# Attention outputs kept in SBUF, a weight ring of three, and the last two gate tiles computed plainly

## The chip, the core and the metric

The kernel runs on one core of a Trainium2 chip. TensorE (PE) does the matmuls, ScalarE (ACT) and VectorE (DVE) the elementwise work beside it, GpSimd (POOL) some elementwise work and DMA issue, and SyncE (SP) issues most DMAs; SP's queue is called SPq in the rows. The metric is the device time of one execution in microseconds (us), as a median of repeated runs.

## The reference

Sequence length S is 512, model width 2048 (16 chunks of 128), all float32. Two layers of a first block are followed by one layer of a second. Cut to what this case touches:

```python
for l in range(2):                                   # first block
    h = rmsnorm(x, attn_norm_g[l])
    qa, ka, va, ga, cq, ckv, kr, gb = split(h @ w_in[l])
    ya = swa_attention(qa, ka, va, sinks[l]) * silu(ga)      # 16 heads, window 128
    yb = mla_attention(cq, ckv, kr, ...) * silu(gb)          # 8 heads of 128
    x = x + concat([ya, yb]) @ w_out[l]
x = rmsnorm(x, final_norm_g)
# second block, 16 meta tokens in front
q, k, v, g_attn, u, g_pool, m_attn, m_pool = split(rmsnorm(hs) @ w_in_2)
o_attn = stick_breaking_attention(q, k, v) * silu(g_attn)
o_pool = (pool(u) @ pool_w) * pool_scale * silu(g_pool)
merged = sigmoid(m_attn) * (o_attn @ w_attn_up) + sigmoid(m_pool) * (o_pool @ w_pool_up)
out = rmsnorm(hs + merged @ w_out_2)
```

## The kernel before

Activations lie transposed: a tile holds 128 features by 512 positions. Every float32 product is made of three matmuls: each operand is split into a high part (a CAST on ACT, names ending in h) and a low part (a subtract on DVE, names ending in l), and `mm3` adds high x high, high x low and low x high. A plain output tile of 128 features takes two weights (halves of the contraction) of 8 chunks each, so 2 x 24 matmuls of 512 columns.

**Weights.** `next_w` keeps two split weights ahead of PE. SP loads each weight (128x1024) into the ring `wr` (four buffers, L179), ACT casts it into `wh` (three buffers), DVE writes `wl` (three buffers). A load into `wr` has to wait until the subtract that reads the old content is done; that subtract follows the cast, and the cast waits until PE has left the weight three places back. SP issues in program order, so a DMA that stands behind a weight load waits with it.

**Slots.** Nearly every other tile comes from one pool, `slots`, of 74 buffers of 128x528.

**Order.** The order in which the program issues work is the order on each engine. GEMMs run as the main line; attention heads (`mla_head`, `swa_pair`) are generators that are stepped between matmuls (`tick`), by a running estimate of PE's time. `SEQ1` lists the tiles of a layer of the first block: after cq, ckv, kr come the eight multi-head-latent heads (tiles gb), whose outputs are called yb (chunks 0 to 7), then ka, va, and the eight sliding-window pairs: a projection qa0, then qa(i), ga(i-1) in turn, then ga7. Pair i is started after qa(i); it computes scores (sc) and probabilities p, transposes them (tp), splits them (pTh, pTl), multiplies with v (o) and, when gate ga(i) is there, copies two halves to `ya` (L531), adds the rest and multiplies by the gate: chunk 8 + i.

`ydst` (L754) sends chunks 0 to 13 of y to DRAM (`yd`) on POOL's queue; only the last two stay. `yget` (L760) reads a chunk back into a tile `yr` through SP, and splits it. It is called for y0 to y7 after ga4 to ga7, two each, and for y8 to y15 when the output projection first needs them. The output projection computes its first three tiles as a group: first half of the contraction (y0 to y7) for three tiles, then the second half (y8 to y15) for three tiles.

**Second block.** `SEQ2`: heads, pool tiles, then the gates ma and mp. Two neighbouring gate tiles are one `run_pair` (L312): seven products of 24 matmuls with 256 columns each (in z, x and y), in place of the 2 x 48 of 512 of two plain tiles. Four of the seven weights are sums of weight blocks that POOL's DMAs made earlier in DRAM (`wsd`, `sum_step`, 16 pairs). The gate's sigmoid (sga) goes to DRAM (`sgd`). The chunks o0 to o15 of the heads and the pool lie in DRAM (`od`); `o_load` (L1110) reads one through SP and splits it. o0 to o7 are loaded after the last pair's matmuls are issued, o8 to o15 behind the pair's gates. Then au(i) (needs o0 to o7) and pu(i) (needs o8 to o15) follow, one weight each.

Of the kernel before, what the change touches and what calls it, by code (L numbers as in the profile page):

```python
# [18 lines left out]
P = 128  # L19
# [16 lines left out]
POOL_W = (2, 4, 8, 16)  # L36

GRP = 3
NSLOT = 74
HN = S // 2  # L40
SUMPAIRS = NC
NSIDE = 3
TP_WAIT = 4000

# [53 lines left out]
def trunk_kernel(ctx, tc, xT, w_in, w_qkv, w_out, w_in2, w_pool, w_aup, w_pup, w_out2, metaT, vec, cst, outT):  # L98
# [9 lines left out]
    def slot(name, dt=F32, cols=S):  # L108
        t = slots.tile([P, W], dt, tag="s", name=name)
        return t[:, :cols]  # L110
# [64 lines left out]
    wq = deque()  # L175
    wready = deque()

    def w_raw(src, n, tag="wr", bufs=4):
        raw = wp.tile([P, WCOLS], F32, tag=tag, name=tag, bufs=bufs)[:, :n]  # L179
        nc.sync.dma_start(raw, src)  # L180
        return raw
# [233 lines left out]
        nc.sync.dma_start(diag_t, cst[:, C_DIAG:C_DIAG + S])  # L415

    xd = [tc.dram_tile([P, NC, S], F32, name=f"xd{i}") for i in range(2)]
    yd = [tc.dram_tile([P, NC, S], F32, name=f"yd{i}") for i in range(2)]

    def split_g(x, g, name):  # L420
        hi = slot(name + "h", F32R)
# [30 lines left out]
    def swa_pair(i, qps, r, st, nsink, gate, ydst):  # L452
        qf = slot("qf")
        stt(qf, qps, 0.125, r, ALU.mult, ALU.mult)
        qs_t = []
        for kv in range(2):
            t = slot("qs", F32R)
            on = slice(kv * 64, kv * 64 + 64)
            off = slice(64 - kv * 64, 128 - kv * 64)
            split(qf[on], "", hi=t[on], lo=t[off])  # L460
            qs_t.append(t)
        al = slot("alibi")
        for kv in range(2):
            nc.gpsimd.tensor_scalar(al[:, kv * 256:(kv + 1) * 256], delta_t, -SLOPES[kv * 8 + i], None, op0=ALU.mult)
        yield 4500
        while "vz" not in st:
            yield 500
        kz, vz = st["kz"], st["vz"]
        nm = small.tile([P, 8], F32, tag="nm", name="nm")
        rs = small.tile([P, 8], F32, tag="rs", name="rs")  # L470
        es = small.tile([P, 8], F32, tag="es", name="es")
        pts = []
        for b in range(NB):
            sc = ps_at("sc")
            c0 = P if b == 0 else 0
            qs = slice(b * P, (b + 1) * P)
            ks = slice(max(b - 1, 0) * P, (b + 1) * P)
            pt = slot("p")
            for kv in range(2):
                kh, kl = kz[kv]  # L480
                js = slice(kv * 256 + c0, kv * 256 + 256)
                mm2(sc[:, js], qs_t[kv][:, qs], kh[:, ks], kl[:, ks], True, True)
            for kv in range(2):
                js = slice(kv * 256 + c0, kv * 256 + 256)
                j = 2 * b + kv
                nc.vector.tensor_tensor_reduce(pt[:, js], sc[:, js], al[:, js], -1.0, nsink[:, 2 * i + kv:2 * i + kv + 1],  # L486
                                               ALU.add, ALU.min, nm[:, j:j + 1])
                act(pt[:, js], pt[:, js], AF.Exp, bias=nm[:, j:j + 1], scale=-1.0, accum_out=rs[:, j:j + 1])
            pts.append(pt)
            yield 1200  # L490
        sk = nsink[:, 2 * i:2 * i + 2].unsqueeze(1).to_broadcast([P, NB, 2])
        tt(es.rearrange("p (b k) -> p b k", k=2), nm.rearrange("p (b k) -> p b k", k=2), sk, ALU.subtract)
        act(es, es, AF.Exp)
        tt(rs, rs, es, ALU.add)
        nc.vector.reciprocal(rs, rs)
        for b in range(NB):
            c0 = P if b == 0 else 0
            v = pts[b].rearrange("p (h k) -> p h k", k=256)[:, :, c0:256]
            nc.vector.tensor_tensor(v, v, rs[:, 2 * b:2 * b + 2].unsqueeze(2).to_broadcast([P, 2, 256 - c0]), ALU.mult)
        yield 4000  # L500
        o = [ps_at("o"), ps_at("o")]
        todo = []

        def pv(j, nq, th, tl, first):
            for kv in range(2):
                cs = slice(kv * nq * P, (kv + 1) * nq * P)
                mm2(o[kv][:, j * P:(j + nq) * P], vz[kv][:, j, :], th[:, cs], tl[:, cs], first, j == 3)

        for j in (0, 2, 1, 3):
            nq = 2 if j < 3 else 1  # L510
            tp = ps_at("tp")
            th = slot("pTh", F32R)
            tl = slot("pTl", F32R)
            for kv in range(2):
                for a in range(nq):
                    src = pts[j + a][:, kv * 256 + (1 - a) * P:kv * 256 + (2 - a) * P]
                    transp(tp[:, (kv * nq + a) * P:(kv * nq + a + 1) * P], src)
            n = 2 * nq * P
            split(tp[:, :n], "", hi=th[:, :n], lo=tl[:, :n])
            if todo:  # L520
                pv(*todo.pop())
            todo.append((j, nq, th, tl, j == 0))
            yield TP_WAIT
        pv(*todo.pop())
        while ("a", i) not in gate:
            yield 500
        y = slot("ya")
        for kv in range(2):
            on = slice(kv * 64, kv * 64 + 64)
            off = slice(64 - kv * 64, 128 - kv * 64)  # L530
            nc.scalar.copy(y[on], o[kv][off])  # L531
            tt(y[on], o[kv][on], y[on], ALU.add)
        nc.gpsimd.tensor_tensor(y, y, gate.pop(("a", i)), ALU.mult)
        ydst(8 + i, y)

    def lora_norm(pss, gcol, name, res):

# [73 lines left out]
    def mla_head(h, pr, kr, gate, ydst):  # L611
# [51 lines left out]
            yield 500  # L663
        y = slot("yb")
        tt(y, o, gate.pop(("b", h)), ALU.mult)
        ydst(h, y)

    def grouped(w, t0, n):
        for u in range(2):
# [3 lines left out]
    def plan():  # L673
# [23 lines left out]
        for kind, i in SEQ2:  # L697
            if kind == "pw":
                wq.append((w_pool[i], 512))
            elif kind == "au":  # L700
                wq.append((w_aup[i], WCOLS))
            elif kind == "pu":
                wq.append((w_pup[i], WCOLS))
            elif kind in ("ma", "mp"):
                if i % 2 == 0:
                    blocks = (w_in2[t, 0], w_in2[t, 1], w_in2[t + 1, 0], w_in2[t + 1, 1])
                    wq.extend((src, WCOLS) for src in pair_steps(len(pairs), *blocks))
                    pairs.append(blocks)
                t += 1
            else:  # L710
                for u in range(2):
                    wq.append((w_in2[t, u], WCOLS))
                t += 1
# [24 lines left out]
    def layer(lay, h, rd, x_src, x_dst):  # L738
# [12 lines left out]
        y = [None] * NC  # L751
        ys = [None] * NC

        def ydst(c, t):  # L754
            if c < NC - 2:
                nc.gpsimd.dma_start(yd[lay][:, c, :], t)
                t = True
            y[c] = t

        def yget(c):  # L760
            if ys[c] is None:
                need(lambda: y[c] is not None)
                t = y[c]
                if t is True:
                    t = slot("yr")
                    nc.sync.dma_start(t, yd[lay][:, c, :])
                ys[c] = split(t, f"y{c}")
                y[c] = None
            return ys[c]

# [5 lines left out]
        for kind, i in SEQ1:  # L776
# [18 lines left out]
            elif kind == "pb":  # L795
                mla_proj_b(st["cqn"], st["ckvn"], proj[i])
                tick()
            elif kind == "pc":
                pr = proj.pop(i)
                mla_proj_c(st["ckvn"], pr)  # L800
                for hh in range(2):
                    start_side(mla_head(2 * i + hh, pr, kr, gate, ydst), 6000 + 3000 * hh)
            elif kind == "ka":
                ka = scaled("kaf")
            elif kind == "va":
                start_side(swa_prep(ka, scaled("vaf"), st))
            elif kind == "qa":
                start_side(swa_pair(i, run_gemm(2, 8, hget), rd["r"], st, nsink, gate, ydst))
            elif kind == "ga":
                gate["a", i] = gate_silu(run_gemm(2, 8, hget), rd["r"], "ga")  # L810
                if i >= 4:
                    yget(2 * i - 8)
                    yget(2 * i - 7)

        sq = SumSq("x")
        if lay == 1:
# [303 lines left out]
    for kind, i in SEQ2:  # L1120
# [21 lines left out]
        elif kind == "pw":  # L1142
            wh, wl = next_w()
            rhs = [pooled.pop(2 * i), pooled.pop(2 * i + 1)]
            for d in range(2):
# [5 lines left out]
                stt(t, ps, vcol(V_PSC + 2 * i + d), gates.pop(("p", 2 * i + d)), ALU.mult, ALU.mult)  # L1151
                nc.sync.dma_start(od[:, SB + 2 * i + d, :], t)
        elif kind in ("ma", "mp"):
            if i % 2:
                continue
            if not oo:
                need(lambda: len(done) == SB)
                oo = [None] * (2 * SB)
            at = i + (0 if kind == "ma" else NC)
            c = run_pair(tset, 8)  # L1160
            if (kind, i) == ("mp", NC - 2):
                X2 = tset = None
                for k in range(SB):
                    oo[k] = o_load(k)
            for d, t in enumerate(pair_out(c, sr)):
                nc.scalar.dma_start(sgd[:, at + d, :], gate_sigmoid(t, "sg"))
            if X2 is None:
                for k in range(SB, 2 * SB):
                    oo[k] = o_load(k)
        elif kind == "au":  # L1170
            ya = slot("ym")
            ga = sg_load(i)
# [180 lines left out]
```

## Time and profile before

| | |
|---|---|
| median of 3 runs | 2760.93 us (2760.64 to 2765.09) |
| the profiled execution | 2759.14 us, span 2757.4 us |
| granted PE clock, mean over the span | 0.991 of full speed |
| busy share of the span | PE 97%, DVE 58%, ACT 44%, POOL 18% |
| DMA traffic | 395.81 MB, 144 GB/s on average |

The span runs from the first to the last instruction of the profiled execution; times in rows are counted from its start. A matmul's duration in the rows includes its way through the array, so the distance from one start to the next is the rate. In a row of the timeline, [2.40 <-ACT pTh L137] says that the engine was idle for 2.40 us before it and that the cast to pTh ended the wait.

### The profile page before, as it was taken

What the parts mean: (1) busy time and instruction counts of PE and PEld (TensorE: products, weight loads), DVE (VectorE), ACT (ScalarE), POOL (GpSimd) and SP (SyncE); (2) the same over time, 40 slices, a digit from 0 to 9 for tenths busy, and PEclk for the clock granted to TensorE, in tenths of its full rate; (3) what the DMA queues carried; (4) which work ended last, traced back from release to release, by engine and by line L of the source; (5) the groups of instructions that cost most, each with busy time, mean ns of one, the idle gap of its engine ahead of it and who ended that gap; (6) DMA issues with size and microseconds to landing.
All of it is one profiled execution on the core that took longest, in us unless ns stands there. A gap on an engine that the chain in (4) does not pass through costs nothing.

```text
span 2757.4 us, 37840 instructions
## 1 busy us (share of the span) xinstructions
PE 2688.1 (97%) x14809; PEld 2315.0 (84%) x14809; DVE 1605.9 (58%) x2399; ACT 1217.0 (44%) x2021; POOL 507.9 (18%) x461
## 2 busy tenths in 40 slices
PE   8999999899999999999999999999999999899997
PEld 6888888688788888877888989898899999688886
DVE  7767567544476756655554444547566666544445
ACT  5445455432344445553334433443346666422232
POOL 4121132222111213223411111111220000011112
PEclk9999999999999999999999999999999999999998
DMA  5354554567654554557632222223346666644334
GB/s 182 114 142 131 138 140 139 168 199 206 174 135 134 141 136 138 150 149 196 188 114 76 77 79 82 70 77 118 100 138 218 208 215 212 199 143 143 120 121 130
DMA packets 129410, 395.81 MB, mean 144 GB/s; under 512 B 14400, under 2 KB 18880, under 8 KB 129232
## 3 DMA queue, kind: packets, MB, share of 16 engines
q1 hardware_dynamic: 103568, 309.90, 35.1%
q0 software_dynamic: 20912, 75.04, 12.5%
q10 hardware_dynamic: 4752, 8.46, 0.8%
q8 instruction: 116, 1.90, 0.3%
q14 instruction: 62, 0.51, 0.1%
HBM read 360.84 MB, written 99.61 MB: 167 GB/s over the span
## 4 chain that ended last, share of the span: by engine, by line
PE 51%; issue 2%; DVE 2%; ACT 1%; POOL 1%; DMA 1%; SPq 0%; DVEq 0%; POOLq 0%; ACTq 0%
PE mm L146 27%; PE mmA L146 5%; PE y L146 5%; PE mmB L146 5%; PE x L146 3%; PE z L146 3%; ACT sp L129 1%; PE so L146 1%; POOL suf L989 0%; DMA ol<-od 0%; DVE out L1231 0%; POOL suf L988 0%; PE pw L146 0%; DVE sufl L122 0%; DMA yr<-yd 0%
## 5 line engine op out<-in xcount | busy, mean ns | idle before, releaser
L218 ACT CAST wh<-wr 128x1024 fp32r<-128x1024 f32 (+2 forms) x496 | 512.0, 1032 | 1001.0 <-PE mm L146 643.7
L122 DVE TENSOR_TENSOR wl<-wr,wh 128x1024 fp32r<-128x1024 f32 (+2 forms) x496 | 637.1, 1286 | 361.1 <-ACT wh L218 344.7
L146 PE MATMUL mm<-hh,wh 128*128 128x512 f32 x1024 | 410.7, 401 | 6.7 <-ACT wh L218 6.5
L146 PE MATMUL mm<-hh,wl 128*128 128x512 f32 x1024 | 405.6, 396 | 4.3 <-DVE wl L122 4.2
L146 PE MATMUL mm<-hl,wh 128*128 128x512 f32 x1024 | 405.6, 396 | 2.2 <-DVE hl L125 2.2
L146 PEld LDWEIGHTS mm<-hh,wl 128*128 128x128 f32 x1024 | 193.4, 189 | 50.3 <-DVE wl L122 5.8
L146 PEld LDWEIGHTS mm<-hh,wh 128*128 128x128 f32 x1024 | 193.8, 189 | 43.0 <-ACT wh L218 6.5
L146 PEld LDWEIGHTS mm<-hl,wh 128*128 128x128 f32 x1024 | 193.6, 189 | 39.8 <-DVE hl L125 4.0
L206 POOL DMA_DIRECT2D wsd<-in_w_in x96 | 62.7, 653 | 500.8 <-PE mm L146 339.6
L146 PE MATMUL mm<-Xh,wh 128*128 128x512 f32 x384 | 152.7, 398 | 0.0
L146 PE MATMUL mm<-Xl,wh 128*128 128x512 f32 x384 | 151.4, 394 | 0.0
L146 PE MATMUL mm<-Xh,wl 128*128 128x512 f32 x384 | 151.1, 394 | 0.0
L1178 POOL TENSOR_TENSOR ym<-ym,yp 128x512 f32<-128x512 f32 x16 | 21.7, 1354 | 489.0 <-DVE yp L122 391.6
L146 PE MATMUL mmA<-Xh,wh 128*128 128x264 f32 x384 | 109.9, 286 | 0.0
L146 PE MATMUL mmB<-Xh,wl 128*128 128x264 f32 x384 | 109.8, 286 | 0.0
L146 PE MATMUL mmB<-Xh,wh 128*128 128x264 f32 x384 | 109.7, 286 | 0.0
L146 PE MATMUL mmB<-Xl,wh 128*128 128x264 f32 x384 | 109.5, 285 | 0.0
L146 PE MATMUL mmA<-Xh,wl 128*128 128x264 f32 x384 | 109.3, 285 | 0.0
L146 PE MATMUL mmA<-Xl,wh 128*128 128x264 f32 x384 | 109.2, 284 | 0.0
L146 PEld LDWEIGHTS mm<-Xh,wl 128*128 128x128 f32 x384 | 72.1, 188 | 16.8
L131 ACT ACTIVATE p<-p,nm 128x256 f32<-128x256 f32 (+1 forms) x128 | 60.7, 475 | 57.6 <-DVE nm L486 56.4
L146 PEld LDWEIGHTS mm<-Xh,wh 128*128 128x128 f32 x384 | 72.2, 188 | 15.0
(874 smaller groups left out, 6951.0 us busy)
## 6 DMA issues: line engine op xcount, KB each, us to landing
wr<-in_w_in SPq DMA_DIRECT2D x272, 512.0 KB, 3.7
wr<-in_w_out SPq DMA_DIRECT2D x100, 512.0 KB, 3.8
wsd<-in_w_in POOLq DMA_DIRECT2D x96, 512.0 KB, 4.6
wr<-wsd SPq DMA_DIRECT2D x64, 512.0 KB, 4.3
wsd<-wsd POOLq DMA_DIRECT2D x32, 512.0 KB, 6.0
xd<-xn SPq DMA_DIRECT2D x32, 256.0 KB, 3.0
sgd<-sga ACTq DMA_DIRECT2D x32, 256.0 KB, 2.9
wr<-in_w_aup SPq DMA_DIRECT2D x16, 512.0 KB, 3.7
```

Of the source, the lines that this page charges most:

```text
L122: nc.vector.tensor_tensor(out, a, b, op)
L129: nc.scalar.activation(out, x, func, bias=bias, scale=scale)
L131: nc.scalar.activation(out, x, func, bias=bias, scale=scale, accum_out=accum_out)
L146: last_pe[0] = nc.tensor.matmul(out, a, b, start=start, stop=stop, skip_group_check=True).ins
L206: i = nc.gpsimd.dma_start(dst, src, **kw)
L218: nc.scalar.copy(hi, raw)
L1178: nc.gpsimd.tensor_tensor(ya, ya, yp, ALU.add)
```

## The change

1. y stays on chip. `ydst` and `yd` are gone; `y[c]` holds the finished tile in its slot, and `yget` splits it from there. The splits of y0 to y7 are called at qa0 to qa7, one each, before the pair is started.
2. The ring `wr` has three buffers in place of four, `slots` 80 in place of 74. A wr buffer is 4096 bytes per partition, a slot 2112.
3. The last mp pair (tiles 14 and 15) is computed as two plain tiles. o0 to o7 are loaded before tile 14, o8 to o15 between tiles 14 and 15. There are sums for 15 pairs in place of 16.

```diff
-NSLOT = 74
+NSLOT = 80
-SUMPAIRS = NC
+SUMPAIRS = NC - 1
...
-    def w_raw(src, n, tag="wr", bufs=4):
+    def w_raw(src, n, tag="wr", bufs=3):
...
-        ydst(8 + i, y)
+        ydst[8 + i] = y
...
-        ydst(h, y)
+        ydst[h] = y
...
             elif kind in ("ma", "mp"):
-                if i % 2 == 0:
+                if (kind, i) >= ("mp", NC - 2):
+                    for u in range(2):
+                        wq.append((w_in2[t, u], WCOLS))
+                elif i % 2 == 0:
...
-        def ydst(c, t):
-            if c < NC - 2:
-                nc.gpsimd.dma_start(yd[lay][:, c, :], t)
-                t = True
-            y[c] = t
-
         def yget(c):
             if ys[c] is None:
                 need(lambda: y[c] is not None)
-                t = y[c]
-                if t is True:
-                    t = slot("yr")
-                    nc.sync.dma_start(t, yd[lay][:, c, :])
-                ys[c] = split(t, f"y{c}")
+                ys[c] = split(y[c], f"y{c}")
                 y[c] = None
             return ys[c]
...
             elif kind == "qa":
-                start_side(swa_pair(i, run_gemm(2, 8, hget), rd["r"], st, nsink, gate, ydst))
+                yget(i)
+                start_side(swa_pair(i, run_gemm(2, 8, hget), rd["r"], st, nsink, gate, y))
             elif kind == "ga":
                 gate["a", i] = gate_silu(run_gemm(2, 8, hget), rd["r"], "ga")
-                if i >= 4:
-                    yget(2 * i - 8)
-                    yget(2 * i - 7)
...
         elif kind in ("ma", "mp"):
+            at = i + (0 if kind == "ma" else NC)
+            if (kind, i) >= ("mp", NC - 2):
+                if i == NC - 2:
+                    tset = None
+                    oo = [o_load(k) for k in range(SB)]
+                t = slot("sg")
+                tt(t, run_gemm(2, 8, x2), sr, ALU.mult)
+                nc.scalar.dma_start(sgd[:, at, :], gate_sigmoid(t, "sg"))
+                if i == NC - 2:
+                    oo += [o_load(k) for k in range(SB, 2 * SB)]
+                else:
+                    X2 = None
+                continue
             if i % 2:
                 continue
-            if not oo:
+            if (kind, i) == ("ma", 0):
                 need(lambda: len(done) == SB)
-                oo = [None] * (2 * SB)
-            at = i + (0 if kind == "ma" else NC)
             c = run_pair(tset, 8)
-            if (kind, i) == ("mp", NC - 2):
-                X2 = tset = None
-                for k in range(SB):
-                    oo[k] = o_load(k)
             for d, t in enumerate(pair_out(c, sr)):
                 nc.scalar.dma_start(sgd[:, at + d, :], gate_sigmoid(t, "sg"))
-            if X2 is None:
-                for k in range(SB, 2 * SB):
-                    oo[k] = o_load(k)
```

How the change moves instructions on ACT and SP is shown by three places. A row is line, operation, output and input, output shape. The first is ACT around gate ga6 of layer 0, in the kernel before: gag is the gate tile, gaa its sigmoid's steps.

```order
L218 CAST wh<-wr 128x1024
L129 ACTIVATE gaa<-gag 128x512
L129 ACTIVATE gaa<-gaa 128x512 x2
L137 CAST y4h<-yr 128x512
L129 ACTIVATE gaa<-gaa 128x512
L218 CAST wh<-wr 128x1024
L137 CAST y5h<-yr 128x512
L531 COPY ya<-o 64x512 x2
L137 CAST pTh<-tp 128x512 x2
L218 CAST wh<-wr 128x1024
```

The same engine in the changed kernel, at the gate of a pair that carries a split (y5):

```order
L218 CAST wh<-wr 128x1024
L129 ACTIVATE gaa<-gag 128x512
L137 CAST y5h<-yb 128x512
L129 ACTIVATE gaa<-gaa 128x512 x2
L530 COPY ya<-o 64x512 x2
L129 ACTIVATE gaa<-gaa 128x512
L137 CAST pTh<-tp 128x512
L218 CAST wh<-wr 128x1024
```

The two copies to ya and the first cast to pTh stood behind a weight cast and two y casts, and now stand ahead of the next weight cast, behind one y cast that reads a tile already in SBUF.

The second place is ACT at the end of layer 0, where the output projection begins; in the kernel before:

```order
L137 CAST y6h<-yr 128x512
L129 ACTIVATE gaa<-gaa 128x512
L137 CAST y7h<-yr 128x512
L137 CAST pTh<-tp 128x512
L137 CAST pTh<-tp 128x256
L218 CAST wh<-wr 128x1024
L531 COPY ya<-o 64x512 x2
L218 CAST wh<-wr 128x1024
L137 CAST y8h<-yr 128x512
L137 CAST y9h<-yr 128x512
L218 CAST wh<-wr 128x1024
L137 CAST y10h<-yr 128x512
```

And in the changed kernel:

```order
L137 CAST pTh<-tp 128x512
L129 ACTIVATE gaa<-gaa 128x512 x3
L137 CAST pTh<-tp 128x256
L218 CAST wh<-wr 128x1024
L530 COPY ya<-o 64x512 x2
L137 CAST y8h<-ya 128x512
L137 CAST y9h<-ya 128x512
L137 CAST y10h<-ya 128x512
L218 CAST wh<-wr 128x1024
L137 CAST y11h<-ya 128x512
L137 CAST y12h<-ya 128x512
```

No cast reads a tile yr any more, y6 and y7 are gone from this place, and y8 to y10 follow the last copies at once.

The third place is SP at the last gate pair. Before, from the first weight of the up-projections on (wr from in_w_aup and in_w_pup; ol are the reads of o):

```order
L180 DMA wr<-in_w_aup 128x1024
L180 DMA wr<-in_w_pup 128x1024
L1112 DMA ol<-od 128x512
L180 DMA wr<-in_w_aup 128x1024
L1112 DMA ol<-od 128x512
L180 DMA wr<-in_w_pup 128x1024
L180 DMA wr<-in_w_aup 128x1024
L1112 DMA ol<-od 128x512
L180 DMA wr<-in_w_pup 128x1024
L1112 DMA ol<-od 128x512
L180 DMA wr<-in_w_aup 128x1024
L1112 DMA ol<-od 128x512 x5
```

In the changed kernel, where four weights of the two plain tiles come just ahead of this:

```order
L180 DMA wr<-in_w_aup 128x1024
L180 DMA wr<-in_w_pup 128x1024
L1102 DMA ol<-od 128x512 x2
L180 DMA wr<-in_w_aup 128x1024
L1102 DMA ol<-od 128x512
L180 DMA wr<-in_w_pup 128x1024
L1102 DMA ol<-od 128x512 x2
L180 DMA wr<-in_w_aup 128x1024
L1102 DMA ol<-od 128x512
L180 DMA wr<-in_w_pup 128x1024
L1102 DMA ol<-od 128x512 x3
L180 DMA wr<-in_w_aup 128x1024
```

Behind these rows stand a weight of pu and seven reads before, and seven reads directly after the last row now. Ahead of o6 to o8 stands the load of the third pu weight.

## Rows read from the trace of the kernel before

**Rows 1.** The page: busy time, share and instructions of each engine.

```profile
PE 2688.1 (97%) x14809; PEld 2315.0 (84%) x14809; DVE 1605.9 (58%) x2399; ACT 1217.0 (44%) x2021; POOL 507.9 (18%) x461
```

**Rows 2.** Waits of PE: total, times, longest, in us.

```profile
PE o L146 <- DVE pTl L122: 6.9, 8, 1.0
...
PE mm L146 <- ACT y11h L137: 5.4, 2, 3.0
```

**Rows 3.** Chain of waits, one plain tile: start, us, what.

```profile
1475.37 11.12 PE mm L146 x48
```

**Rows 4.** Timeline of PE, end of layer 0: start, us, instruction, idle before.

```profile
515.85 0.35 PE L146 MATMUL o<-pTh,vz 128*128 128x256 f32 x1 [0.24 <-DVE ya L122]
517.21 0.39 PE L146 MATMUL o<-pTl,vz 128*128 128x256 f32 x1 [1.00 <-DVE pTl L122]
...
528.34 0.38 PE L146 MATMUL o<-pTh,vz 128*128 128x256 f32 x1 [2.40 <-ACT pTh L137]
...
542.58 0.39 PE L146 MATMUL mm<-y8h,wh 128*128 128x512 f32 x1
...
555.99 0.39 PE L146 MATMUL mm<-y8h,wh 128*128 128x512 f32 x1
```

**Rows 5.** Timeline of ACT: pair 3, end of layer 0, end of layer 1.

```profile
422.94 0.58 ACT L531 COPY ya<-o 64x512 f32<-64x512 f32 x1
...
426.12 1.05 ACT L218 CAST wh<-wr 128x1024 fp32r<-128x1024 f32 x1
...
512.20 1.05 ACT L218 CAST wh<-wr 128x1024 fp32r<-128x1024 f32 x1 [1.64 <-PE mm L146]
...
513.79 1.19 ACT L531 COPY ya<-o 64x512 f32<-64x512 f32 x2
...
527.18 0.62 ACT L137 CAST y7h<-yr 128x512 fp32r<-128x512 f32 x1 [2.45 <-DMA yr<-yd]
...
1230.27 1.19 ACT L531 COPY ya<-o 64x512 f32<-64x512 f32 x2 [2.58 <-PE o L146]
```

**Rows 6.** Timeline of PE, end of layer 1.

```profile
1222.87 0.39 PE L146 MATMUL o<-pTh,vz 128*128 128x256 f32 x1 [2.52 <-ACT pTh L137]
...
1224.26 0.63 PE L146 MATMUL mm<-y6h,wh 128*128 128x512 f32 x1
...
1227.82 0.39 PE L146 MATMUL mm<-y1h,wh 128*128 128x512 f32 x1
...
1238.68 0.39 PE L146 MATMUL mm<-y8h,wh 128*128 128x512 f32 x1
...
1252.16 0.40 PE L146 MATMUL mm<-y8h,wh 128*128 128x512 f32 x1
```

**Rows 7.** Timeline of PE: last gate pair, au0, and au1 behind pu0.

```profile
2343.68 0.28 PE L146 MATMUL z<-t12h,wh 128*128 128x256 f32 x1
...
2363.49 0.39 PE L146 MATMUL mm<-o0h,wh 128*128 128x512 f32 x1
...
2393.49 0.40 PE L146 MATMUL mm<-o0h,wh 128*128 128x512 f32 x1
```

**Rows 8.** Chain of waits through au0 and pu0: start, us, what.

```profile
2366.28 4.86 DMA ol<-od
...
2377.22 1.05 ACT wh L218
...
2378.30 1.24 DVE wl L122
...
2383.34 7.47 DMA ol<-od
```

**Rows 9.** Busy time by stretch: us, PE, PEld, DVE, ACT, POOL, PEclk, DMA share, GB/s.

```profile
2060.00:2340.00 280.00, 280.00 (x2377) 280.00 (x2376) 188.96 (x242) 173.06 (x239) 0.00 (x0) 1.00 0.68 213
```

**Rows 10.** The page, DMA issues: count, KB each, us to landing.

```profile
wr<-wsd SPq DMA_DIRECT2D x64, 512.0 KB, 4.3
```

More of the change, by code (lines that the diff above doesn't have):

```diff
@@ L417, in trunk_kernel @@
     xd = [tc.dram_tile([P, NC, S], F32, name=f"xd{i}") for i in range(2)]
-    yd = [tc.dram_tile([P, NC, S], F32, name=f"yd{i}") for i in range(2)]
     def split_g(x, g, name):
@@ L801, in layer @@
                 for hh in range(2):
-                    start_side(mla_head(2 * i + hh, pr, kr, gate, ydst), 6000 + 3000 * hh)
+                    start_side(mla_head(2 * i + hh, pr, kr, gate, y), 6000 + 3000 * hh)
             elif kind == "ka":
```

## The prediction

> **What bounds the kernel now.** I read the page first. TensorE (PE) is busy 97% of the span [rows 1], so a change can gain only where PE idles, where it runs at half clock, or where matmuls go away. Next came PE's list of waits: pTl of the sliding-window pairs leads it, and y11h of the output projection stands near the top [rows 2], both of them tiles near the edits. Then I went to those places in the timeline. At full clock 48 matmuls of 512 columns take 11.12 us, so one takes 0.2317 and the 24 of one weight 5.56 [rows 3].
>
> *Layer 0 tail* [rows 4]. PE idles 0.24 us for ya and then 1.00 for pTl, here and in the two pairs before. Over both layers pTl's 6.9 us in 8 waits [rows 2] are six of 1.00 and two of 0.46. At 528.34 comes 2.40 for pTh and then one of the two 0.46. The first output tile reaches y8 at 542.58 and its 24 matmuls end at 555.99: 13.41 us instead of 5.56, because y10 and y11 come late, 5.4 us for y11h over both layers [rows 2], and the clock then falls to its lower level.
>
> ScalarE shows why [rows 5]. At 512.20 a weight cast (wh) that had to wait 1.64 us for PE stands ahead of the copies to ya and of pTh. At 527.18 the cast y7h waits 2.45 for the read-back of y (yr<-yd), and pTh is queued behind it. In pair 3, which has no y split, the copy at 422.94 stands ahead of the weight cast at 426.12, and PE shows no idle time there.
>
> *Layer 1 tail* [rows 6]. The same: three pairs, 2.52 at 1222.87 (and the other 0.46 for pTl), then nine matmuls mostly at half clock (0.63 in the rows where it is 0.39 at full clock), and y8 to the tile's end from 1238.68 to 1252.16.
>
> *Last gate pair and first up-projections* [rows 7]. The pair starts at 2343.68, au0 at 2363.49, and pu0 ends at 2393.49, though au0 and pu0 together need 11.12. The chain of waits runs through reads of o that stand in SP's queue behind weight loads [rows 8].
>
> **The change part by part.**
>
> *y stays on chip.* The 28 writes yd<-y on POOL's queue and the 28 reads on SP's go away. A y split is now a cast from a tile that was finished long before, and it stands in another place: ScalarE's order of the change puts one y cast among the gate's activations and both copies to ya ahead of the weight cast, as in pair 3 of before. So I take the whole 1.24 of six pairs as gone. The split itself (a cast of 0.62 us, and on DVE a subtract half as wide as a weight's 1.24 [rows 8]) falls into ScalarE's idle 1.64 [rows 5]. Bounds: gain 0 if that split delays pTl as the old place did, 7.4 (6 x 1.24) if not. I take the upper end, because pair 3 has that order and no wait. y7h no longer waits for a DMA, and nothing else stood between pTh and its transposes.
>
> At the tail, y8 to y15 now follow the last copies, at 1230.27 + 1.19 = 1231.5 [rows 5]. Eight casts of 0.62 and one weight cast of 1.05 are 6.0 us, so they end near 1237.5, and PE needs y8 at 1238.68 [rows 6], y15 4.9 us later. Nothing is late there; if it were, the first to wait would be y15, by its subtract.
>
> Layer 0: 3 x 1.24 + 2.40 + 0.46 + (13.41 - 5.56) = 3.72 + 2.86 + 7.85 = 14.4 us.
> Layer 1: 3.72 + 2.52 + 0.46, plus nine matmuls from 1224.26 to 1227.82 (3.56 against 2.09, so 1.47), plus 13.48 - 5.56 = 7.92: 16.1 us.
>
> *wr ring of three.* A load now waits for the subtract three weights earlier, not four. This bites where weights go fastest, in the gate pairs: one each 2.83 us (a pair of seven takes 19.81 [rows 7]). PE shows no idle from 2060 to 2340 [rows 9]. Three casts are 8.5 us apart; cast and subtract of the old weight take 1.05 + 1.24 [rows 8]; a load from wsd lands in 4.3 [rows 10]. So 8.5 - 2.3 - 4.3 = 1.9 us remain before a cast is late, and PE then still has two weights (5.66) against cast and subtract (2.3): 3.4 more. Cost 0; without that cover, each microsecond beyond 5.3 counts on up to 105 weights. With 5.56-us weights the cover is over 10 us. At the start, the fifth load waits for one more subtract; I take 0.3 for it, between 0 and one subtract (1.24).
>
> *Slots and sums.* Six more slots, eight fewer POOL sums: nothing on PE's path, 0.
>
> *Last mp pair plain, o read earlier.* Two tiles of 11.12 replace 19.81: +2.43 [rows 3, 7]. Count from the start of tile 14. Before, au0 ended at 2377.22 - 2343.68 = 33.5 (ScalarE's cast starts on its release [rows 8]), and from there to pu0's end were 16.3. After, au0 starts at 22.2 and reaches o6 at 26.4. But SP issues o6 to o8 behind the load of the third pu weight, which waits for the subtract of a1, whose cast waits for PE to leave the last plain weight, at 22.2. Cast, subtract and issue put the read at 25.0 (1.05 + 1.24 + two issues); with the 4.86 of o4's read [rows 8] it lands at 29.9, and the cast makes o6 ready at 30.5. PE idles 4 us and then has six matmuls, 1.4 at full clock and 2.8 at half of it: au0 ends at 31.9 to 33.3, a gain of 0.2 to 1.6. Behind it the order is the old one (a weight load, then seven reads, o15 last), so 16.3 stay. I take +1.0. Bounds: a read as slow as the chain's 7.47 [rows 8] makes it -2; no wait at all in au0 makes it +5.7.
>
> The Trainium skill's page "DMA: Bandwidth & Descriptors", section "Anatomy of one DMA", gives a transfer 2.0 us plus its bytes at 436 GB/s, measured on GpSimd's queue. An estimate from it for 256 KB is 2.6 us, and with that the sum would be 2.3 us larger. This trace disagrees with it for these reads (4.86, and 7.47 with more of them in the queue [rows 8]), so the rows are used.
>
> **Sum.** 14.4 + 16.1 + 1.0 - 0.3 = 31.2 us. The profiled run took 2759.14, 1.8 below the median of the runs; the stalls are the same size in either, so I subtract from the median: 2760.93 - 31.2 = 2729.7.
>
> **Rivals.**
> *Part of the stalls stays* (0.14). One y split now sits in each of 14 pairs instead of 8 in the last ones. If it holds pTl up as before, 7.4 stay; if also one tail's y wait stays, 7.9 more. Gain 16 to 24, time 2737 to 2745. For it: each old stall is 1 us, about the length of one split. Against: pair 3's order.
> *Place 3 goes better* (0.06): o6 arrives in time, or the clock does not fall: 2722 to 2726. Against: a read of 4.86 us where one of some 0.8 would do.
> *The change doesn't do what it says* (0.06). Up to 14 y tiles stay in slots and only six slots are added; if tiles of the pairs wait for slots, each of 14 pairs loses 1 to 2 us and the gain shrinks to between 16 and nothing: 2745 to 2760. Half of this lies within 0.2%. For it: the arithmetic 14 against 6. Against: nothing waits for a slot on PE's list now.
> *Slower: the ring of three starves PE in the gate pairs* (0.04). 31.2 over 105 weights is 0.30 us each, so it decides once a load with its wait takes 4.3 + 5.3 + 0.3 = 9.9 us; at 10.1 the time is 2760.93 - 31.2 + 105 x 0.5 = 2782. For it: the DMA engines are 68% busy there [rows 9]. Against: reads of 9.9 us appear nowhere in that stage.
>
> **How the numbers follow.** The forecast has 0.70, with 2725 to 2734 as its own range (-2 to +5.7 of place 3 with 3 us of the pairs). What a measurement of this kernel can tell from no change is about 0.2%, 5.5 us. Faster: 0.70 + 0.14 + 0.06 + half of 0.06 = 0.93; same 0.03; slower 0.04. The range takes in the forecast and most of the first rival: 2724 to 2743.
>
> **What would show it.** Right: PE's list no longer names pTl at 1.0, pTh, y10h or y11h; the first output tile's second half takes 5.6 us per weight in both layers; PE has no idle in 2060 to 2340; au0 still waits for o6 some 4 us. Wrong: waits for wl or wh in the gate pairs, pTl waits of 1 us in all pairs, or y tiles that wait for the last copies.

## The result, and the profile after

The changed kernel takes 2719.5 us as a median of 4 runs (2718.8 to 2723.6), beside 2762.8 for the kernel before in the same comparison: ratio 0.9846, interval 0.9829 to 0.9863. The profiled execution took 2723.55, against 2759.14. A second measurement, below, gave 2721.9 against 2760.1, ratio 0.9861 (0.9848 to 0.9875). So the gain is 38 to 43 us in the timed runs and 35.6 between the two profiled ones. The forecast was 31.2, and the time lies below its range.

PE's list of waits (total, times, longest) had, beside pTl and y11h of [rows 2], these two before:

```profile
PE o L146 <- ACT pTh L137: 4.9, 2, 2.5
...
PE mm L146 <- ACT y10h L137: 3.1, 2, 1.9
```

None of the four is in the changed kernel's list:

```profile
PE mm L146 <- ACT wh L218: 6.7, 1, 6.7
...
PE mm L146 <- ACT o8h L137: 3.1, 1, 3.1
PE mm L146 <- ACT o6h L137: 2.9, 1, 2.9
...
PE csum L146 <- ACT csh L137: 2.2, 1, 2.2
PE mm L146 <- ACT o9h L137: 1.8, 1, 1.8
```

The first, 6.7 us at the start of the program, was there before at 6.5. Busy time by stretch (columns as in [rows 9]): both layer tails are now full, and the gate pairs stay without idle time on a ring of three.

```profile
500.00:600.00 100.00, 100.00 (x450) 81.55 (x449) 54.86 (x64) 41.22 (x64) 24.38 (x22) 1.00 0.69 188
1200.00:1300.00 100.00, 100.00 (x440) 81.41 (x439) 55.86 (x61) 40.29 (x62) 33.25 (x27) 1.00 0.58 172
2030.00:2300.00 270.00, 270.00 (x2286) 270.00 (x2285) 181.47 (x231) 169.20 (x236) 0.00 (x0) 1.00 0.68 213
```

ACT at the gate whose copies fed the waits of [rows 4] and [rows 5]: the copies to ya stand ahead of the weight cast, as the listing of the order showed.

```profile
504.64 0.58 ACT L530 COPY ya<-o 64x512 f32<-64x512 f32 x1
...
508.31 0.57 ACT L137 CAST pTh<-tp 128x512 fp32r<-128x512 f32 x1
508.99 1.05 ACT L218 CAST wh<-wr 128x1024 fp32r<-128x1024 f32 x1
```

The first two matmuls of [rows 4], with the transposes (tp) ahead of them and the matmul behind them; first in the kernel before, then in the changed one:

```profile
515.01 0.60 PE L150 MATMUL tp<-ident,p 128*128 128x128 f32 x4
...
517.43 0.28 PE L146 MATMUL o<-pTh,vz 128*128 128x256 f32 x1
```

```profile
511.81 0.60 PE L150 MATMUL tp<-ident,p 128*128 128x128 f32 x4
512.17 0.37 PE L146 MATMUL o<-pTh,vz 128*128 128x256 f32 x1
512.37 0.28 PE L146 MATMUL o<-pTl,vz 128*128 128x256 f32 x1
512.49 0.28 PE L146 MATMUL o<-pTh,vz 128*128 128x256 f32 x1
...
534.21 0.40 PE L146 MATMUL mm<-y8h,wh 128*128 128x512 f32 x1
...
539.80 0.40 PE L146 MATMUL mm<-y8h,wh 128*128 128x512 f32 x1
```

The last two rows are the first output tile's y8: 5.59 us from one start to the next, 13.41 before.

Here lies the surprise. From pTh to pTl it is 0.20 us now and was 1.36, so this wait gave back 1.16, not the 1.00 that the row marked as idle. From the start of the tp group to pTh it is 0.36 now, where it was 0.84: 0.48 came back for a marked 0.24. From pTl to the next matmul it is 0.12, where it was 0.22. Together the pair gave back 1.74.

PE at the last plain tile, au0 and pu0 (the first row starts tile 14, the last one au1 behind pu0), for [rows 7]:

```profile
2310.18 0.39 PE L146 MATMUL mm<-Xh,wh 128*128 128x512 f32 x1
...
2339.65 0.80 PE L146 MATMUL mm<-o6h,wh 128*128 128x512 f32 x1 [2.91 <-ACT o6h L137]
...
2345.95 0.80 PE L146 MATMUL mm<-o8h,wh 128*128 128x512 f32 x1 [3.07 <-ACT o8h L137]
...
2349.82 0.80 PE L146 MATMUL mm<-o9h,wh 128*128 128x512 f32 x1 [1.83 <-ACT o9h L137]
...
2357.99 0.40 PE L146 MATMUL mm<-o0h,wh 128*128 128x512 f32 x1
```

From the pair's or tile 14's start to the end of pu0 it is 47.8 us now and was 49.8.

Since PE runs the same matmuls in the same order outside the last gate pair, the start of each can be set against its start before. The table gives, for six stretches of the span (bounds in the first kernel's time), how much the second kernel gains or loses within it; minus is faster. The second column compares two experiments, told below, that differ only in part 1 of the change: where y is kept and where it is split.

```
stretch                          before -> changed   room_only -> y_room
450-520   three pairs, layer 0         -5.24               -5.09
520-540   late pair, layer 0           -3.40               -6.08
540-560   y8 to y15, layer 0           -7.85               -8.39
700-740   layer boundary               +2.96               +0.49
1140-1256 pairs and tail, layer 1     -18.38              -17.79
1400-2055 block 2, same work           -2.14               -0.30
```

The lines for the two layer tails add up to 34.9 us in the first column and 37.4 in the second; the forecast had 14.4 + 16.1 = 30.5 for them.

### The profile page after: what moved, and what is told of

Read it like the earlier page. It is cut to its first block, busy times and chain, and to the rows that moved or that the text cites. A ratio compares the mean times of both kernels' runs of the same rounds, so it can differ in the third digit from the quotient of the medians.

```text
span 2721.8 us, 37412 instructions
## 1 busy us (share of the span) xinstructions
PE 2676.3 (98%) x14737; PEld 2309.3 (85%) x14737; DVE 1598.8 (59%) x2390; ACT 1211.2 (45%) x2016; POOL 487.7 (18%) x425
## 4 chain that ended last, share of the span: by engine, by line
PE 90%; DVE 3%; issue 3%; ACT 2%; POOL 1%; DMA 1%; SPq 0%; DVEq 0%; POOLq 0%; ACTq 0%
PE mm L146 59%; PE mmA L146 5%; PE y L146 5%; PE mmB L146 5%; PE x L146 3%; PE z L146 3%; PE msc L146 1%; PE qn L146 1%; PE sc L146 1%; PE o L146 1%; PE mo L146 1%; PE tp L150 1%; ACT sp L129 1%; PE kn L146 1%; PE qr L146 1%
## 5 line engine op out<-in xcount | busy, mean ns | idle before, releaser
L146 PEld LDWEIGHTS mm<-hh,wh 128*128 128x128 f32 x1024 | 194.1, 190 | 43.3 <-ACT wh L218 6.7
L146 PE MATMUL mm<-Xh,wh 128*128 128x512 f32 x416 | 165.1, 397 | 0.0
L146 PE MATMUL mm<-Xh,wl 128*128 128x512 f32 x416 | 163.9, 394 | 0.0
L146 PE MATMUL mm<-Xl,wh 128*128 128x512 f32 x416 | 163.6, 393 | 0.0
L146 PEld LDWEIGHTS mm<-Xh,wl 128*128 128x128 f32 x416 | 78.1, 188 | 18.1
L146 PEld LDWEIGHTS mm<-Xl,wh 128*128 128x128 f32 x416 | 78.2, 188 | 16.4
L146 PEld LDWEIGHTS mm<-Xh,wh 128*128 128x128 f32 x416 | 78.3, 188 | 16.1
```

Of the source, the lines that this page charges most:

```text
L146: last_pe[0] = nc.tensor.matmul(out, a, b, start=start, stop=stop, skip_group_check=True).ins
```

## The experiments

Four of them cut the change into its parts; parts 1, 2 and 3 are those of the list in the section on the change. Ratios are those to the kernel before, measured beside each experiment, with their intervals. The runs fall into three sets: the first four experiments, the next four, and the last four. The median of the kernel before was 2759.3 in the first, 2762.7 in the second and 2760.1 in the third, so a difference of 2 or 3 us between times of different sets tells little.

**y alone (y_only).** Part 1 on the kernel before, whole; 74 slots and four wr buffers stay:

```diff
-        ydst(h, y)
+        ydst[h] = y
...
-                t = y[c]
-                if t is True:
-                    t = slot("yr")
-                    nc.sync.dma_start(t, yd[lay][:, c, :])
-                ys[c] = split(t, f"y{c}")
+                ys[c] = split(y[c], f"y{c}")
...
             elif kind == "qa":
+                yget(i)
```

> The kernel before with y kept on chip and one split per pair, but with 74 slots and four wr buffers, and the last gate pair as it was. Theory A (the gain lies in the two layer tails, where a stall costs more than its marked idle: 1.74 us instead of 1.24 for each pTl, 35 us in all; slots and ring are only room): 35 us less than before, and no wait for pTl, pTh, y10h or y11h on PE. Theory B (the six slots are needed, since up to 14 y tiles stay): the pairs wait for slots, and the gain is under 20 us.

Measured: 2722.6, ratio 0.9871 (0.9858 to 0.9885), 36.7 us less; none of the four waits is in PE's list. That is theory A. Theory B, one of the forecast's rivals, falls: 74 slots sufficed.

**Room alone (room_only).**

```diff
-NSLOT = 74
+NSLOT = 80
...
-    def w_raw(src, n, tag="wr", bufs=4):
+    def w_raw(src, n, tag="wr", bufs=3):
```

> The kernel before with 80 slots and three wr buffers, nothing else. Theory A: no difference, within 2 us of before, and no wait for wh or wl in the gate pairs. Theory C (the ring or the slots give part of the surplus over the forecast): 5 to 10 us less than before.

Measured: 2756.9, ratio 0.9990 (0.9981 to 0.9999), 2.4 us less. The interval just leaves out 1. In the trace the gate pairs show no wait, as said for theory A, and the two traces end level (0.05 us apart): block 2 from 1400 to 2055 and au0 with pu0 are each 1.9 shorter than in the trace of before, and the late pair of layer 0 (2.7) and the boundary of the layers (2.2), with half clock behind them here, take as much back. au0 and pu0 are 1.4 shorter in y_only too, which has no room. Whether the room gives the timed 2 us stays open. This trace showed something else, PE's timeline at the wait of 528.34 in [rows 4]:

```profile
528.15 0.58 PE L146 MATMUL o<-pTh,vz 128*128 128x256 f32 x1 [2.42 <-ACT pTh L137]
...
529.80 0.63 PE L146 MATMUL mm<-y6h,wh 128*128 128x512 f32 x1
530.22 0.63 PE L146 MATMUL mm<-y6l,wh 128*128 128x512 f32 x1
...
534.06 0.63 PE L146 MATMUL mm<-y1l,wh 128*128 128x512 f32 x1
534.49 0.56 PE L146 MATMUL mm<-y1h,wl 128*128 128x512 f32 x1
534.89 0.39 PE L146 MATMUL mm<-y2h,wh 128*128 128x512 f32 x1
```

The same wait of 2.4 us is followed here by half clock (0.63 per row, 0.43 from start to start) until 534.9. In the trace on which the forecast was made the clock stayed full there. That is the difference between 3.40 and 6.08 in the table.

**The last gate pair alone (plain_only).** Part 3 on the kernel before, whole, as in the diff of the change.

> The kernel before with only the last mp pair computed plainly and the o reads issued earlier. Theory A: 1 to 3 us less than before (in the changed kernel's trace the offset moves by 1.9 us over this stretch). Theory C (the surplus over the forecast lies here): 8 to 12 us less. With 74 slots the reads of o8 to o15 could wait for slots; then it is up to 3 us slower than before.

Measured: 2758.8, ratio 0.9999 (0.9990 to 1.0007), 0.4 us less. PE waits there for o6h (3.0), o8h (3.1) and o9h (1.8), as in the changed kernel. The gain is below the 1 to 3 of theory A, not clear of nothing, and far from theory C.

**All but the last gate pair (y_room).** Parts 1 and 2.

> The changed kernel with the last gate pair as it was before: y on chip, three wr buffers, 80 slots. Theory A: 35 to 39 us less than before, 2 us more than the changed kernel. Theory C (the surplus lies in the last gate tiles): 31 us less than before.

Measured: 2721.0, ratio 0.9864 (0.9848 to 0.9880), 38.3 us less, theory A. Of the changed kernel's two medians one is 1.5 us below this, the other 0.9 above it. So part 3 is worth at most some 2 us and nothing that these runs can tell from none, and the gain is part 1: y_only, with part 1 alone, has 36.7 of it.

**Where the splits stand (qa_place, ga_place).** First the kernel before, y still read back, with only this edit; then the changed kernel with the reverse one:

```diff
             elif kind == "qa":
+                yget(i)
...
-                if i >= 4:
-                    yget(2 * i - 8)
-                    yget(2 * i - 7)
```

> The kernel before (y still goes to DRAM and is read back) with the splits of y0 to y7 called at qa0 to qa7, one each. Theory A (the pTl and pTh waits come from where the splits stand; only the waits for y10 and y11 come from the read-back): pTl's waits of 1.0 and the pTh waits of 2.4 go, y10h and y11h stay; 17 to 20 us less than before. Theory D (the read-back is at the root of all of them): under 5 us less.

Measured: 2741.7, ratio 0.9923 (0.9909 to 0.9936), 21.0 us less. Of PE's list there:

```profile
PE mm L146 <- ACT y11h L137: 5.4, 2, 2.8
...
PE mm L146 <- ACT y10h L137: 3.2, 2, 1.7
...
PE o L146 <- DVE pTl L122: 1.0, 2, 0.6
```

y10h and y11h are as before, six of the eight pTl waits are gone, and pTh is out of the list. That is theory A; the time is 1 us better than its range.

> The changed kernel with the splits of y0 to y7 back at ga4 to ga7, two each, y on chip as it is. Theory A: the six waits for pTl come back, at 1.7 us each from start to start, so 10 us more than the changed kernel, 2729 to 2731, and no wait for y10h or y11h. Theory D: no such wait, within 2 us of the changed kernel.

Measured: 2721.0, ratio 0.9851 (0.9838 to 0.9865): the same as the changed kernel, with no pTl in the list. Theory A is wrong in this point, and theory D holds. ACT's order at the gate with y4 and y5 reads there:

```
L129 ACTIVATE gaa<-gag 128x512
L137 CAST y4h<-yb 128x512
L129 ACTIVATE gaa<-gaa 128x512 x2
L137 CAST y5h<-yb 128x512
L530 COPY ya<-o 64x512
L129 ACTIVATE gaa<-gaa 128x512
L530 COPY ya<-o 64x512
L137 CAST pTh<-tp 128x512
L218 CAST wh<-wr 128x1024
```

Two splits of tiles on chip go ahead of the weight cast. In the kernel before, the second split stood behind it, and the copies behind that. So neither the place nor the read-back alone makes the pairs wait: only the two together put the copies behind the weight cast, and either edit cures it. ACT itself waits for a read only from y7 on (2.45 us in [rows 5]) and not for y0 to y6, so for the six pairs the cause that these runs show is the order. Only keeping y on chip cures the waits for y10 and y11.

**The layer boundary (meta_early).** A small read (metas, 128 KB) stands at the boundary, and the split for the column sum (csum) stands behind it. The table's +2.96 at 700 to 740 comes from there. The chain of waits of the changed kernel shows the read, and PE's timeline the sum and the matmuls behind it:

```profile
697.16 7.66 DMA metas<-in_metaT
```

```profile
705.88 0.49 PE L146 MATMUL csum<-csh,ones_r 128*128 128x512 f32 x1 [2.25 <-ACT csh L137]
...
707.64 0.63 PE L146 MATMUL mm<-hh,wh 128*128 128x512 f32 x1
```

In the trace of before the wait was 0.9 us and the clock stayed full. The edit, on the changed kernel:

```diff
+    metas = const.tile([P, NM * NC], F32, name="metas")
+    nc.gpsimd.dma_start(metas, metaT)
     h, rd = layer(0, h, rd, xT, xd[0])
-    metas = slot("metas", F32, NM * NC)
-    nc.sync.dma_start(metas, metaT)
```

> The changed kernel with the small read of metas issued before layer 0 on another queue, into a tile of its own. Theory E (the part of the time that differs from run to run lies at the boundary of the layers, where the column sum waits for that read and the clock may fall behind it): PE's wait for csh at the boundary goes, 2 to 4 us less than the changed kernel, and its runs lie closer together. Rival: nothing changes, because POOL's sum of xq is as late as the read.

Measured: 2717.4, ratio 0.9838 (0.9825 to 0.9852), 3.7 us below ga_place, which ran beside it and is as fast as the changed kernel. The wait for csh is out of PE's list, and in this trace the clock stays full there. The runs lie no closer together (2716.3 to 2720.4, against 2718.8 to 2723.6), so that half of theory E is not borne out.

**The reads of o (o_pool).**

```diff
         t = slot("ol")
-        nc.sync.dma_start(t, od[:, c, :])
+        nc.gpsimd.dma_start(t, od[:, c, :])
```

> The changed kernel with the reads of o issued on POOL's queue, where no weight load stands ahead of them. Theory F (au0 and pu0 lose 13 to 14 us to waits and half clock, all because the reads stand behind weight loads): au0 and pu0 run at full clock, 9 to 14 us less than the changed kernel. Rival G (the reads wait for slots that only the last plain tile frees, or the DMA engines are full): o0 to o7 come in time, o8 to o15 don't, 3 to 6 us less.

Measured: 2714.0, ratio 0.9822 (0.9808 to 0.9835), 7.0 us below ga_place, and 5.5 below the first median of the changed kernel. au0 waits for nothing; pu0 waits 4.6 for o8h. The size is nearer to rival G than to theory F, but its reason isn't the right one: the reads were issued from 2274.3 to 2319.1, that of o8 first in the row below, and ACT's timeline has the cast of o8 34 us later, behind a weight cast and the activations of tile 14's gate.

```profile
2305.11 2.65 POOL L1102 DMA_DIRECT2D ol<-od  x5 [8.29 <-DVE c L122]
```

```profile
2334.79 1.04 ACT L218 CAST wh<-wr 128x1024 fp32r<-128x1024 f32 x1 [2.92 <-PE mm L146]
2335.74 0.63 ACT L129 ACTIVATE sga<-sg 128x512 f32<-128x512 f32 x1
2336.40 1.29 ACT L129 ACTIVATE sga<-sga 128x512 f32<-128x512 f32 x2
2338.45 0.63 ACT L129 ACTIVATE sga<-sga 128x512 f32<-128x512 f32 x1 [0.76 <-DVE sga L125]
2338.99 0.60 ACT L137 CAST o8h<-ol 128x512 fp32r<-128x512 f32 x1
```

**The last four** were measured beside the same 9 runs of before, with a median of 2760.1. First the changed kernel again (after_again).

> The changed kernel once more, beside the same runs of before as the three that follow, and with a second trace. Theory A: 38 to 41 us less than before. Theory H (the first comparison's 43 us was the size): 42 to 44 us less.

Measured: 2721.9, ratio 0.9861, 38.2 us less: theory A. The 5 us between the two comparisons come from both sides: in the first, the median of before was 2.7 higher and that of the changed kernel 2.4 lower.

Then parts 1 and 3 without part 2 (y_plain): y on chip and the plain tiles, with 74 slots and four wr buffers.

> y on chip and the last gate pair plain, but 74 slots and four wr buffers. Theory A (the room is not what the gain needs): within 2 us of the changed kernel. Theory B (part 3 needs the slots, since o0 to o15 and the X2 tiles lie there together): 3 us or more above the changed kernel, with waits for o9 to o15 in pu0.

Measured: 2720.6, ratio 0.9856 (0.9842 to 0.9869), 1.3 us below the changed kernel beside it: theory A. The gain needs no room.

Then o_pool and meta_early together (o_pool_meta).

> The changed kernel with both edits tried alone before: the reads of o on POOL's queue and the read of metas ahead of layer 0. The two lie far apart in the program, so the gains should add: 7 to 9 us less than the changed kernel. Rival: less than 6, if the clock takes one of them back elsewhere.

Measured: 2711.5, ratio 0.9822 (0.9809 to 0.9836), 10.5 us below the changed kernel beside it, more than the 7 to 9 expected. Against ga_place the two edits alone gave 3.7 and 7.0, so they add.

Last, with the splits of o8 to o15 ahead of tile 14's gate (o_pool_early):

```diff
-                t = slot("sg")
-                tt(t, run_gemm(2, 8, x2), sr, ALU.mult)
-                nc.scalar.dma_start(sgd[:, at, :], gate_sigmoid(t, "sg"))
+                ps = run_gemm(2, 8, x2)
                 if i == NC - 2:
                     oo += [o_load(k) for k in range(SB, 2 * SB)]
...
+                t = slot("sg")
+                tt(t, ps, sr, ALU.mult)
+                nc.scalar.dma_start(sgd[:, at, :], gate_sigmoid(t, "sg"))
```

> As the one before, and the splits of o8 to o15 issued ahead of tile 14's gate instead of behind it, so that ScalarE's cast of o8 no longer stands behind four activations of the gate. Theory I (in the run with POOL's queue pu0's wait of 4.65 us is ScalarE's order, not the read): the wait for o8h falls to about 1.7 us (one weight cast and one cast), and the time is 3 to 6 us below the one before. Rival: the wait stays above 4 us, because the reads of o8 to o15 are late themselves.

Measured: 2708.35 (2708.2 to 2708.6), ratio 0.9812 (0.9799 to 0.9825): 3.1 us below the one before it, 13.6 below the changed kernel, 51.7 below the kernel before. That is theory I, at the lower end of its 3 to 6 us: the wait for o8h is 1.42, and 0.85 for o8l follows. PE's timeline, pu0 (the cast of o8 still waits for one weight cast; the clock still falls to half, but from 2337.1 to 2340.5 only, where it was 6.8 us in the run before):

```profile
2334.51 0.49 PE L146 MATMUL mm<-o8h,wh 128*128 128x512 f32 x1 [1.42 <-ACT o8h L137]
2335.86 0.50 PE L146 MATMUL mm<-o8l,wh 128*128 128x512 f32 x1 [0.85 <-DVE o8l L122]
...
2337.54 0.63 PE L146 MATMUL mm<-o10l,wh 128*128 128x512 f32 x1
```

## Why the prediction was wrong

The direction, the places and the cause were right; the sum was too small. Two steps failed: the price of a wait on PE, taken from the idle time that a row marks, and the clock behind the waits, taken from one trace. The range, 2724 to 2743, covered neither: its lower end is place 3 at its best, +5.7 for +1.0, and 1 us more, and the pairs' 7.4 had been called a bound.

**Pairs, 6 x 1.24 = 7.4: the term that was mis-sized.** The forecast added the idle times that the rows mark. A row's idle time is counted from the end of the matmul ahead, and rows of matmuls that follow at once overlap: the pTh row lasts 0.37 us in the changed kernel, and the next start comes 0.20 after its own. From start to start each of the six cost 0.48 + 1.16 + 0.10 = 1.74, and the table's first line has 5.24 for three: 10.5 for six. For the late pairs the forecast had 2.86 and 4.45; from start to start they are 3.4 and 5.1. Where it did count from start to start, it was right: 7.85 and 7.92 for the y8 tiles, 7.82 and 7.93 measured. A seventh wait for ya, 0.31 us at 346.95 in the trace of before, went unnoticed; it gave back some 0.6. So priced, the sum is some 36 instead of 31.2, and the time 2725, still inside the range; the rest is the clock.

**The clock.** The forecast took the one trace's clock as given. In two other traces with the same wait (room_only, plain_only) the clock fell behind 528, which costs 1.2 to 2.7 us more; with it the tails gain 37.4 instead of 34.9 in the table, and the sum of 36 becomes 38.6, or 2722. The boundary of the layers goes the other way: there the trace of before is the exception. Of the eleven traces with the read of metas in its old place, nine, the changed kernel's among them, fell to half clock for 3.4 us, behind waits for csh of 1.5 to 2.8 us; before (0.9) and o_pool (1.1) did not. The start of the program differs as well: from 28 to 36 us the granted clock is 0.57 of full speed in the changed kernel's trace and 1.00 in that of ga_place, and the two are 2.7 us apart in the first 100 us. So the profiled run of the changed kernel had bad luck: its granted clock is 0.992, and its time 2723.6; the other three of its runs had 0.994 to 0.995 and took 2718.8 to 2719.6. Against the trace of before it loses 1.2 at the start and 3.0 at the boundary, most of why the two profiled runs differ by less (35.6) than the timed ones.

**Place 3, +1.0.** Measured 2.0 between the two traces, but traces without part 3 (y_room, y_only, room_only) gain 1.4 to 2.4 there too, and the timed runs can't tell it from nothing. That the +1.0 lies between these is luck. The steps held: o6 to o8 were issued 24.9 us after tile 14's start (forecast 25.0), au0 ended at 32.3 (31.9 to 33.3, counted as there from the start of ScalarE's cast), and the seven reads after it were unchanged. The read took 3.84 where 4.86 had been taken (chain of waits: `2335.12 3.84 DMA ol<-od`). By the Trainium skill's page "DMA: Bandwidth & Descriptors", section "Anatomy of one DMA", an estimate is 2.0 us and the bytes at 436 GB/s, 2.6; this trace disagrees too, and so does that of o_pool, where the reads are on GpSimd's queue as in the page's fit: 3.0 to 8.3 us from issue to landing, with a median of 4.8.

**Ring of three, 0.** Right: the gate pairs still have no idle time (270 of 270 us busy, above), and room_only isn't slower. **Slots, 0.** Right: even 74 are enough. **Start, -0.3.** PE's first wait was 6.7 after 6.5 before, within what the traces of all kernels show (6.3 to 6.7), so the cost can't be told from nothing.

**The rivals.** That part of the stalls stays: no; a y split in every pair holds nothing up. The reason given against it, pair 3's order, was the right one to look at. Place 3 goes better: no; au0 waits 2.9 us for o6, and the clock falls. Pairs that wait for slots, and a ring of three that starves PE: no; 74 slots are enough, and the gate pairs have no idle time.

**What stays open.** Some 2 us between 1400 and 2055, where nothing was changed, are in the comparison with the trace of before and hardly in that of other traces (0.3 in the table). It is a property of that one execution; what of, no run here shows. The pieces shown, 35 to 37 us for the tails and up to 2 for part 3, make 35 to 39. That reaches the 38.2 of the larger comparison. The 43.3 of the first one rests on four runs of each kernel, and its surplus was not traced; how often the clock falls in the timed runs without a trace isn't shown either.

## What to carry to other kernels

Price a wait on PE from start to start, against the same instructions where they don't wait, and not by the idle time of the row: here that is 1.74 against 1.24 for each pair's wait. Price what follows each long wait twice, with the clock full and with the clock at half, since one trace shows only one of the two. And where a cast waits behind work of another chain, look at the engine's order first: the reads of o were made early twice (part 3, and POOL's queue), and 3 us more came only when the casts were moved.

## What the runs showed of the hardware that was not expected

The same wait of 2.4 us before the same matmul was followed by full clock in one execution and by half clock for 6 us in another, 0.39 against 0.63 us per matmul row. Beside each other, nine executions of the kernel before lie 5.6 us apart (2758.3 to 2763.8), and four of the last variant, which has fewer waits of this kind, 0.4 us. The granted clock goes with it: among the 21 runs of before in the first set the two with 0.988 took 2763.5 and 2764.1 us, the three with 0.992 took 2756.3 to 2758.3. That the clock is the cause of all of the spread is still an inference.
